# A feed-forward up product by seven products of quarters, with the down product in a stage of its own

## The chip, the cores and the metric

The kernel runs on one core of a Trainium2 chip. The metric is the time of one execution on the device in microseconds (us). The engines of the core work side by side, each through its own queue in order: TensorE (PE) multiplies, VectorE (DVE), ScalarE (ACT) and GpSimd (POOL) work elementwise, and SyncE (SP) issues the DMAs. A matmul holds one 128x128 block of weights, loaded just before it (PEld in the profile), and streams the columns of the other operand through it. Results come up in PSUM and are taken from there to SBUF by DVE or ACT.

## The reference

One layer of a hybrid decoder, in float32: an mLSTM branch, an SSD branch, a merge, a LayerNorm, and a feed-forward part with a short causal convolution. The change touches only the last part (1056 token columns after the cut of the meta tokens, width 1024, inner width 2816):

```python
x1 = layer_norm(ALPHA * x + mixed, w['ln1_g'], w['ln1_b'])
up = x1 @ w['w_up']                                   # 1024 -> 2 * 2816
upc, fconv_new = causal_dwconv(up, fconv_buf, w['w_fconv'], w['b_fconv'])
ff = (jax.nn.silu(upc[..., :D_FF]) * upc[..., D_FF:]) @ w['w_down']
x2 = layer_norm(ALPHA * x1 + ff, w['ln2_g'], w['ln2_b'])
```

The layer's output x2 and all convolution and recurrent states are returned.

## The kernel before

Features lie on the 128 partitions and tokens in the free dimension. A float32 operand enters a product as a pair: `hi` is the value rounded for the multiplier (an ACT copy, line 141), `lo` the rest (a DVE subtraction, line 142). Each block product is three matmuls, hi·hi, lo·hi and hi·lo (`mm3`, lines 156 to 158), each with its own weight load.

The normalised activations x1 stand as eight pairs `x1h`, `x1l` (one for each block of 128 features), 1058 columns wide, cut into three column tiles of 354, 352 and 352 (`NTC`). The feed-forward part runs over 22 pairs of units: `act_tile(i)` takes up unit i (the gated half) and unit 22 + i (the other half). An up unit loads a 128x1024 block of `w_up`, splits it into `whi`, `wlo`, and does 3 column tiles x 8 feature blocks x 3 = 72 matmuls; ACT copies the result from PSUM (`gps`) to `u`. Then the convolution runs along the tokens: one ACT pass (line 1092) and two DVE passes (line 1094) a unit; tanh on ACT (line 1104), one DVE pass for the silu (line 1105), and the product of both halves on DVE (lines 1110 and 1111). The result is split at once into `ah`, `al` (`split` in `act_tile`) and kept in SBUF.

The down product runs between the up units. `FPARTS` cuts the 22 activation tiles into parts of 3 or 2; as soon as a part is there, `down` multiplies it with its block of `w_down` into eight output tiles `mix` (`acc`), and after each part DVE adds the PSUM result to them (`down_evac`, 192 additions of 352 columns). A pair that is computed while `down` of the part ahead runs keeps PE supplied. The last part ends with the second LayerNorm. POOL does only small copies in this stage (lines 1075, 1088, 1089). The order on each queue follows the order of the code, except that weight loads (`wload`, `wdn`) are pulled ahead by `WAHEAD` instructions; `wst`, `whi` and `wlo` have two buffers each.

Of the kernel before, what the change touches and what calls it, by code (L numbers as in the profile page):

```python
# [34 lines left out]
FPARTS = [3, 3, 3, 3, 3, 2, 2, 3]  # L35
# [11 lines left out]
def kernel(ctx, tc, I, O):  # L47
# [8 lines left out]
    dr = ctx.enter_context(tc.tile_pool(name="dr", bufs=1, space=DRAM))  # L56

# [12 lines left out]
    rd = dr.tile([4, TC], F32, name="rd")  # L70
    negMd = dr.tile([4, T], F32, name="negMd")
# [19 lines left out]
    maskA = const.tile([NA, NA], F32, name="maskA")  # L91
# [13 lines left out]
    bm = const.tile([96, NB], F32, name="bm")  # L105
# [8 lines left out]
    tk1 = const.tile([128, 9, 12], F32, name="tk1")  # L114
    tk2 = const.tile([128, 9, 96], F32, name="tk2")
    mdec = const.tile([128, 4, 16], F32, name="mdec")
    sdec = const.tile([128, 32, 16], F32, name="sdec")
# [785 lines left out]
    pp = ctx.enter_context(tc.tile_pool(name="pp", bufs=1))  # L903
# [5 lines left out]
    def ptile(dt, nm, w=TC):  # L909
        return pp.tile([128, PW], dt, tag="P", name=nm, bufs=22)[:, 0:w]  # L910

    def pair(src, mul=None):
        f = ptile(F32, "pf")
        dma(f, src)
        if mul is not None:
            V.tensor_tensor(f, f, mul, ALU.mult)
        return pair_of(f)

    def pair_of(f):
        hi, lo = ptile(F32R, "ph"), ptile(F32R, "pl")  # L920
        split(hi, lo, f)
        return hi, lo
# [6 lines left out]
    xp_cm.__exit__(None, None, None)  # L929

    qp_ = ctx.enter_context(tc.tile_pool(name="qmix", bufs=1, side="right"))
    mix = [qp_.tile([128, TC], F32, name=f"mix{m}") for m in range(8)]
    with ExitStack() as c3:
        q2 = c3.enter_context(tc.tile_pool(name="q2", bufs=2, side="right"))

        def gate_tile(m):
            t = q2.tile([128, TC], F32, tag="gt", name="gt")
            dma(t, gd[m])
            return t

        def w3(nm, *ix, **kw):
            src = I[nm]
            for i in ix:
                src = src[i]
            return wload(src.rearrange("p (k c) -> p k c", c=128), **kw)

        def gemms(unit, rhs):
            gemm_wide([unit(0), unit(1)], NTC, rhs)
            for m in range(2, 7):
                w, evac = unit(m)  # L950
                gemm(w, NTC, rhs, evac, KD, gps if m % 2 else rps)
            gemm_wide([unit(7)], NTC, rhs)

        def unit_a(m):
            w = w3("wpa", m, scale=mg)
            gt = gate_tile(m)

            def evac(j, t0, n, ps, gt=gt, m=m):
                V.scalar_tensor_tensor(mix[m][:, t0:t0 + n], gt[:, t0:t0 + n], 1.0, ps, op0=ALU.add, op1=ALU.mult)
            return w, evac  # L960
        gemms(unit_a, prhs(hp))
        for half in range(2):
            yp = []
            for k in range(8):
                if k % 4 == 0:
                    R = q2.tile([128, TC], F32, tag="R", name="R")
                    gi = half * 2 + k // 4
                    dma(R, rd[gi:gi + 1].rearrange("o t -> (o t)").partition_broadcast(128))
                yp.append(pair(yd[half * 8 + k], mul=R))

            def unit_b(m):
                w = w3("wpb", m, half, scale=sg[:, half * 8:half * 8 + 8])
                gt = gate_tile(8 + m)

                def evac(j, t0, n, ps, gt=gt, m=m):
                    tmp = q2.tile([128, 354], F32, tag="tmp", name="tmp")
                    V.scalar_tensor_tensor(tmp[:, 0:n], gt[:, t0:t0 + n], 1.0, ps, op0=ALU.add, op1=ALU.mult)
                    V.tensor_tensor(mix[m][:, t0:t0 + n], mix[m][:, t0:t0 + n], tmp[:, 0:n], ALU.add)
                return w, evac
            gemms(unit_b, prhs(yp))  # L980
    mpair = [pair_of(mix[k]) for k in range(8)]
    x1x = ctx.enter_context(tc.tile_pool(name="x1x", bufs=1, side="right"))

    def x1tile(k, nm):
        return ptile(F32R, nm) if k < 3 else x1x.tile([128, TC], F32R, name=f"{nm}{k}")

    with ExitStack() as c3:
        q3 = c3.enter_context(tc.tile_pool(name="q3", bufs=2, side="right"))
        x1p = [(x1tile(k, "x1h"), x1tile(k, "x1l")) for k in range(8)]
        def unit_out(m, t0, n, s1=None):  # L990
            w = wload(I["wout"][m].rearrange("p (k c) -> p k c", c=128))
            xr = q3.tile([128, 354], F32, tag="tmp", name="xr")
            dma(xr[:, 0:n], xd[m, :, t0:t0 + n])

            def evac(_, t0, n, ps):
                r = mix[m][:, t0:t0 + n]
                V.scalar_tensor_tensor(r, ps, 0.5 / ALPHA, xr[:, 0:n], op0=ALU.mult, op1=ALU.add)
                if m:
                    G.tensor_tensor(s1[:, 0:n], mix[0][:, t0:t0 + n] if m == 1 else s1[:, 0:n], r, ALU.add)
            return w, evac  # L1000

        def parts(n):
            return [(a, min(128, n - a)) for a in range(0, n, 128)]

# [92 lines left out]
    def act_tile(i):  # L1097
# [8 lines left out]
        if i:  # L1106
            next(ub)
# [204 lines left out]
```

## Time and profile before

| | us |
|---|---|
| median of 3 runs (lowest to highest) | 2491.01 (2485.77 to 2493.09) |
| the profiled execution | 2483.84 |
| its span, first to last instruction | 2481.9 |
| PE busy in the span | 2410.1 |
| DVE busy | 1464.1 |
| ACT busy | 837.5 |
| POOL busy | 382.4 |
| from the first matmul on x1 (1664.5) to the last (2386.7) | 722.2 |

A matmul's busy time reaches from its start to its modelled end and overlaps the next one's. What a matmul costs is read from the distance of starts. Idle time of an engine is put down to the instruction that released it.

### The profile page before, as it was taken

What the parts mean: (1) busy time and instruction counts of PE and PEld (TensorE: products, weight loads), DVE (VectorE), ACT (ScalarE), POOL (GpSimd) and SP (SyncE); (2) the same over time, 40 slices, a digit from 0 to 9 for tenths busy, and PEclk for the clock granted to TensorE, in tenths of its full rate; (3) what the DMA queues carried; (4) which work ended last, traced back from release to release, by engine and by line L of the source; (5) the groups of instructions that cost most, each with busy time, mean ns of one, the idle gap of its engine ahead of it and who ended that gap; (6) DMA issues with size and microseconds to landing.
All of it is one profiled execution on the core that took longest, in us unless ns stands there. A gap on an engine that the chain in (4) does not pass through costs nothing.

```text
span 2481.9 us, 37118 instructions
## 1 busy us (share of the span) xinstructions
PE 2410.1 (97%) x14835; PEld 2300.5 (93%) x14835; DVE 1464.1 (59%) x2449; ACT 837.5 (34%) x1631; POOL 382.4 (15%) x475
## 2 busy tenths in 40 slices
PE   7999999999999999999979999999999999999996
PEld 6898998989999899899979999989999999999995
DVE  7647666567457657654444755686544545445458
ACT  6243332544324424433221211354232323323321
POOL 0010000233123223222000000231010101101104
PEclk9999999999999999999989999999999999999998
DMA  9233332234443353344243433441111111111121
GB/s 245 70 107 116 116 98 85 74 118 113 113 163 75 98 163 74 98 144 118 91 170 132 165 113 104 143 143 40 49 40 50 43 52 44 49 48 44 49 56 70
DMA packets 161853, 241.02 MB, mean 97 GB/s; under 512 B 37433, under 2 KB 117145, under 8 KB 161681
## 3 DMA queue, kind: packets, MB, share of 16 engines
q1 hardware_dynamic: 161680, 238.66, 31.8%
q8 instruction: 116, 1.90, 0.3%
q14 instruction: 57, 0.46, 0.1%
HBM read 188.54 MB, written 50.07 MB: 96 GB/s over the span
## 4 chain that ended last, share of the span: by engine, by line
PE 72%; DVE 3%; DMA 3%; ACT 1%; POOL 1%; issue 0%; SPq 0%; ACTq 0%; POOLq 0%; DVEq 0%
PE gps L156 17%; PE gps L158 17%; PE gps L157 17%; PE rps L158 5%; PE rps L156 5%; PE rps L157 5%; PE rps L787 1%; PE rps L797 1%; PE rps L806 1%; DMA s<-in_s0T 1%; PE rps L713 1%; POOL sqa L1020 1%; DMA out_sS<-s 1%; ACT whi L141 0%; PE rps L749 0%; DMA pf<-yd 0%
## 5 line engine op out<-in xcount | busy, mean ns | idle before, releaser
L156 PE MATMUL gps<-xh,whi 128*128 128x352 f32 (+4 forms) x1752 | 590.8, 337 | 0.0
L157 PE MATMUL gps<-xl,whi 128*128 128x352 f32 (+4 forms) x1752 | 572.8, 327 | 0.0
L158 PE MATMUL gps<-xh,wlo 128*128 128x352 f32 (+4 forms) x1752 | 572.5, 327 | 0.0
L142 DVE TENSOR_TENSOR wlo<-wst,whi 128x1024 fp32r<-128x1024 f32 (+2 forms) x205 | 250.1, 1222 | 404.8 <-ACT whi L141 404.6
L141 ACT ACTIVATE whi<-wst 128x1024 fp32r<-128x1024 f32 (+2 forms) x205 | 207.6, 1015 | 603.8 <-PE gps L157 356.0
L156 PEld LDWEIGHTS gps<-xh,whi 128*128 128x128 f32 (+1 forms) x1752 | 330.7, 189 | 16.4 <-issue 12.4
L156 PE MATMUL gps<-x1h,whi 128*128 128x352 f32 (+1 forms) x1056 | 345.7, 327 | 0.0
L158 PE MATMUL gps<-x1h,wlo 128*128 128x352 f32 (+1 forms) x1056 | 343.7, 325 | 0.0
L157 PE MATMUL gps<-x1l,whi 128*128 128x352 f32 (+1 forms) x1056 | 343.5, 325 | 0.0
L157 PEld LDWEIGHTS gps<-xl,whi 128*128 128x128 f32 (+1 forms) x1752 | 331.0, 189 | 12.5 <-issue 11.8
L158 PEld LDWEIGHTS gps<-xh,wlo 128*128 128x128 f32 (+1 forms) x1752 | 330.1, 188 | 1.1 <-issue 1.0
L158 PEld LDWEIGHTS gps<-x1h,wlo 128*128 128x128 f32 x1056 | 200.6, 190 | 0.1
L157 PEld LDWEIGHTS gps<-x1l,whi 128*128 128x128 f32 x1056 | 200.3, 190 | 0.0
L156 PEld LDWEIGHTS gps<-x1h,whi 128*128 128x128 f32 x1056 | 199.5, 189 | 0.3 <-ACT whi L141 0.2
L156 PE MATMUL gps<-ph,whi 128*128 128x352 f32 (+1 forms) x472 | 151.9, 330 | 9.6 <-ACT ph L141 7.0
L157 PE MATMUL gps<-pl,whi 128*128 128x352 f32 (+1 forms) x472 | 154.5, 327 | 0.0
L158 PE MATMUL gps<-ph,wlo 128*128 128x352 f32 (+1 forms) x472 | 153.4, 326 | 0.0
L708 ACT ACTIVATE dec<-dec,tk 128x128 f32<-128x128 f32 (+1 forms) x288 | 90.3, 383 | 175.8 <-POOL dec L705 153.6
L158 PE MATMUL rps<-ah,wlo 128*128 128x352 f32 x456 | 147.6, 324 | 0.0
L156 PE MATMUL rps<-ah,whi 128*128 128x352 f32 x456 | 147.3, 323 | 0.0
L157 PE MATMUL rps<-al,whi 128*128 128x352 f32 x456 | 147.2, 323 | 0.0
L1119 DVE SCALAR_TENSOR_TENSOR mix<-rps,mix 128x352 f32<-128x352 f32 x168 | 85.3, 521 | 68.7 <-PE rps L158 68.7
(362 smaller groups left out, 4122.9 us busy)
## 6 DMA issues: line engine op xcount, KB each, us to landing
wst<-in_win SPq DMA_DIRECT2D x72, 512.0 KB, 3.7
wst<-in_wup SPq DMA_DIRECT2D x44, 512.0 KB, 3.3
dec<-btd SPq DMA_DIRECT2D x32, 512.0 KB, 5.7
gt<-gd SPq DMA_DIRECT2D x24, 529.0 KB, 3.5
wst<-in_wout SPq DMA_DIRECT2D x24, 512.0 KB, 3.2
wst<-in_wdn SPq DMA_DIRECT2D x24, 384.0 KB, 3.5
yd<-xs SPq DMA_DIRECT2D x16, 529.0 KB, 3.9
pf<-yd SPq DMA_DIRECT2D x16, 529.0 KB, 5.8
```

The lines of the kernel that those rows point to most:

```text
L141: S.activation(hi, src, AF.Copy)
L142: V.tensor_tensor(lo, src, hi.bitcast(F32), ALU.subtract)
L156: PE.matmul(out, ah, bh, start=start, stop=False)
L157: PE.matmul(out, ah, bl, start=False, stop=False)
L158: PE.matmul(out, al, bh, start=False, stop=stop)
L708: S.activation(dec[:n, i, 0:n], dec[:n, i, 0:n], AF.Exp, bias=tk2[:n, c, g * 8 + i:g * 8 + i + 1], scale=1.0)
L713: PE.transpose(xps[:n, i * 128:(i + 1) * 128], xc, ident)
L787: PE.matmul(iv[(i % 2) * 64:(i % 2) * 64 + 64, i // 2, 0:n], xdt[:n, i, :], dec[:n, i, 0:n], start=True, stop=True)
L797: PE.matmul(ev_[:, i, :], St[:, i * 128:(i + 1) * 128], C[:, t0:t0 + n], start=True, stop=True)
L806: PE.matmul(aps, bt_, xw.rearrange("p h e -> p (h e)"), start=True, stop=True)
L1020: G.tensor_tensor(sqa[:, 0:n], sqa[:, 0:n], sq[:, 0:n], ALU.add)
L1119: V.scalar_tensor_tensor(a, ps, 1.0 / ALPHA, a, op0=ALU.mult, op1=ALU.add)
```

## The change

The first two pairs of units (`PLAIN = 2`) are computed as before. For the other 20 pairs the weights of a pair are a 2x2 arrangement of blocks (units i and 22 + i by the two halves of the 1024 features), and x1 a 2x2 arrangement (the halves of the features by two halves of the columns, `HC = 530` each). The pair then takes seven products of such quarters, in the Winograd form: each has 4 feature blocks x 3 matmuls on two column pieces (`HP`, 266 and 264), 168 matmuls a pair. Four products run on a combination of weights (`s1` to `s4`, four POOL operations of 128x512, then a split into `wf`), three on a piece of the weights itself (`a11`, `a12`, `a22`, split straight from the loaded block `raw`). Three run on combinations of x1, which are formed and split once (`tf`), between the LayerNorm and the first of the seven products. Three of the seven products accumulate in a PSUM bank in which another product already lies. The seven results are put together by ACT copies, DVE additions from PSUM and two POOL additions. Weights are prepared five products ahead (`AHEAD`), in six buffers `wf`. The convolution of pair i runs piecewise while pair i + 1 is multiplied (`act_steps`).

The loaded blocks `raw` are the four tiles that first hold the units of the plain pairs. The activations go to DRAM (`fd`) instead of being split at once, and x1 goes there too (`x1d`), since its tiles `mix` serve the new stage as work space. After all up units the down product runs alone: activations are loaded again and split (`act_load`), x1 is loaded into `acc`, and parts of 6, 6, 6 and 4 tiles follow each other, the last as before. The additions to `acc` fall from 192 to 96. Pools of SBUF are arranged anew (`pa`, `pb`, fixed tiles for what stood in `q2`, `q3`, `fp`; three buffers of `tmp`), and the merge's code ahead of the LayerNorm is the same work in other tiles.

```diff
-FPARTS = [3, 3, 3, 3, 3, 2, 2, 3]
+HC = 530
+HP = [(0, 266), (266, 264)]
+PLAIN = 2
+AHEAD = 5
+FPARTS = [6, 6, 6, 4]
...
+    for m in range(8):
+        dma(x1d[m], mix[m][:, 2:TC])
...
+    raws = [ptile(F32, "raw", PW) for _ in range(4)]
+    ca, cb, ta, sw1, sw2, X, uA, uB = mix_
...
+    plains = [plain(m, u) for m, u in zip((0, 22, 1, 23), raws)]
...
+    for k in range(4):
+        b11, b12 = mix_[k][:, 0:HC], mix_[k][:, HC:2 * HC]
+        b21, b22 = mix_[4 + k][:, 0:HC], mix_[4 + k][:, HC:2 * HC]
+        G.tensor_tensor(b11, b12, b11, ALU.subtract)
+        G.tensor_tensor(b12, b22, b12, ALU.subtract)
+        V.tensor_tensor(b22, b22, b11, ALU.subtract)
+        V.tensor_tensor(b21, b22, b21, ALU.subtract)
+        for f, t in enumerate((b11, b22, b12)):
+            split(tf[f][k // 2][0][:, k % 2], tf[f][k // 2][1][:, k % 2], t)
+    for k in range(4):
+        split(x1p[k][0][:, HC:2 * HC], x1p[k][1][:, HC:2 * HC], mix_[4 + k][:, 0:HC])
+    for i in range(PLAIN):
+        run(act_steps(i, *raws[2 * i:2 * i + 2]))
...
+    PRODUCTS = [("a11", half(0, 0)), ("s1", form(0)), ("s2", form(1)), ("s4", half(4, 1)),
+                ("a12", half(4, 0)), ("s3", form(2)), ("a22", half(0, 1))]
...
+    def prepare(n):
...
+        if p == 5 and i < 21:
+            up_load(i + 1)
...
+        if nm == "s1":
+            G.tensor_tensor(t, a21, a22, ALU.add)
+        elif nm == "s2":
+            G.tensor_tensor(t, sums["s1"], a11, ALU.subtract)
+        elif nm == "s4":
+            G.tensor_tensor(t, a12, sums["s2"], ALU.subtract)
+        else:
+            G.tensor_tensor(t, a11, a21, ALU.subtract)
+        split(h, l, t)
...
+    for i in range(PLAIN, 22):
+        for p, (nm, xf) in enumerate(PRODUCTS):
+            n = 7 * (i - PLAIN) + p
+            prepare(n + AHEAD)
...
+                    PE.matmul(ps, wh_, a, start=new and k == 0, stop=False, **chk)
+                    PE.matmul(ps, wh_, b, start=False, stop=False, **chk)
+                    PE.matmul(ps, wl_, a, start=False, stop=k == 3, **chk)
+                s1, s5 = X[:, j, 0:w_], X[:, 2 + j, 0:w_]
+                if p == 0:
+                    S.copy(s1, ps)
+                elif p == 1:
+                    S.copy(s5, ps)
+                elif p == 2:
...
+                    V.tensor_tensor(u2, ps, s1, ALU.add)
+                elif p == 3:
+                    V.tensor_tensor(uA[:, 16 + HC + t0:16 + HC + t0 + w_], ps, banks["u2", j], ALU.add)
+                elif p == 4:
+                    put_copy(uA, t0, w_, ps)
+                elif p == 5:
+                    V.tensor_tensor(s1, ps, s1, ALU.add)
+                    G.tensor_tensor(uB[:, 16 + HC + t0:16 + HC + t0 + w_], s1, s5, ALU.add)
+                else:
+                    put(lambda to, a, b, f: V.tensor_tensor(
+                        to, f(s1[:, a:b]) if f else s1[:, a:b], f(ps[:, a:b]) if f else ps[:, a:b],
+                        ALU.subtract), uB, t0, w_)
...
+    acc = [t[:, 0:TF] for t in (mix_[3:] + mix_[0:3])]
+    for m in range(8):
+        dma(acc[m], x1d[m])
...
+    for kk, nk in zip(FPARTS, FPARTS[1:]):
+        nxt = []
+        for m in range(8):
+            hi, lo = wdn(m, k0, kk, 1)
+            gemm((hi[:, 0], lo[:, 0]), NTF, prhs(acts), down_evac(m), kk, rps if m % 2 else gps)
+            if m < nk:
+                nxt.append(act_load(k0 + kk + m))
+        k0 += kk
+        acts = nxt
```

**TensorE, within the up product.** Each row is a line, an operation, its result and operands, and the columns. Before, two feature blocks at the end of one column tile of a unit:

```order
L156 MATMUL gps<-x1h_14795,whi 128x354
L157 MATMUL gps<-x1l_14796,whi 128x354
L158 MATMUL gps<-x1h_14795,wlo 128x354
L156 MATMUL gps<-x1h_14797,whi 128x354
L157 MATMUL gps<-x1l_14798,whi 128x354
L158 MATMUL gps<-x1h_14797,wlo 128x354
```

After, the end of the first product of the first pair (on x1 itself) and the start of the second (on a combination):

```order
L1253 MATMUL rps<-x1h,wf 128x264
L1254 MATMUL rps<-x1l,wf 128x264
L1255 MATMUL rps<-x1h,wf 128x264
L1253 MATMUL rps<-tf,wf 128x266
L1254 MATMUL rps<-tf,wf 128x266
L1255 MATMUL rps<-tf,wf 128x266
```

The kinds of matmul are the same three; each weight load now serves 264 or 266 columns instead of 352 or 354.

**VectorE, in the middle of the up units.** Before, one pair of units, from the split of its first weights to that of its result (`ca`, `cb`: the two convolutions):

```order
L142 TENSOR_TENSOR wlo<-wst,whi 128x1024
L1094 SCALAR_TENSOR_TENSOR ca<-u,c_fcw,ca 128x1072 x2
L1105 SCALAR_TENSOR_TENSOR ca<-ta,ca 128x1072
L142 TENSOR_TENSOR wlo<-wst,whi 128x1024
L1094 SCALAR_TENSOR_TENSOR cb<-u,c_fcw,cb 128x1072 x2
L1110 TENSOR_TENSOR ta<-ca,cb 128x1024
L1111 TENSOR_TENSOR ta<-ca,cb 128x32
L142 TENSOR_TENSOR al<-ta,ah 128x1056
```

After, half a pair, from the second convolution of the pair ahead to the put-together of the fourth product (L153 is the split, L1119 the convolution, L1130 the product of the halves):

```order
L153 TENSOR_TENSOR wf<-mix,wf 128x512
L1119 SCALAR_TENSOR_TENSOR mix<-mix,c_fcw 128x1072
L153 TENSOR_TENSOR wf<-raw,wf 128x512
L1119 SCALAR_TENSOR_TENSOR mix<-mix,c_fcw 128x1072
L1130 TENSOR_TENSOR mix<-mix 128x1024
L153 TENSOR_TENSOR wf<-raw,wf 128x512
L1131 TENSOR_TENSOR mix<-mix 128x32
L1264 TENSOR_TENSOR tmp<-rps,mix 128x266
L1264 TENSOR_TENSOR tmp<-gps,mix 128x264
L153 TENSOR_TENSOR wf<-mix,wf 128x512
L1266 TENSOR_TENSOR mix<-rps,tmp 128x266
L1266 TENSOR_TENSOR mix<-rps,tmp 128x264
```

The splits of weights are cut in seven smaller ones a pair, the split of the result is gone from this stage, and additions from PSUM stand between the convolutions.

**GpSimd, one pair.** Before, it had three copies a unit (lines 1075, 1088, 1089) and nothing else in this stage. After, one pair of units:

```order
L1215 TENSOR_TENSOR mix<-raw 128x512
L1113 COPY so<-mix 128x2
L1217 TENSOR_TENSOR mix<-mix,raw 128x512
L1114 COPY so<-mix 128x16
L1219 TENSOR_TENSOR mix<-raw,mix 128x512
L1271 TENSOR_TENSOR mix<-mix 128x266
L1271 TENSOR_TENSOR mix<-mix 128x264
L1113 COPY so<-mix 128x2
L1106 COPY mix<-si 128x8x2
L1114 COPY so<-mix 128x16
L1221 TENSOR_TENSOR mix<-raw 128x512
L1106 COPY mix<-si 128x8x2
```

Six operations with two operands in SBUF are new; the six copies of a pair remain.

**VectorE, from the combinations of x1 to the first weights of the seven products** (after only; before, the splits of x1 are followed by the weights and convolutions of the first units):

```order
L1164 TENSOR_TENSOR mix<-mix 128x530
L153 TENSOR_TENSOR tf<-mix,tf 128x530 x2
L1165 TENSOR_TENSOR mix<-mix 128x530
L153 TENSOR_TENSOR tf<-mix,tf 128x530 x2
L1119 SCALAR_TENSOR_TENSOR mix<-raw,c_fcw,mix 128x1072 x4
L1126 SCALAR_TENSOR_TENSOR mix<-mix 128x1072
L1130 TENSOR_TENSOR mix<-mix 128x1024
L1131 TENSOR_TENSOR mix<-mix 128x32
L153 TENSOR_TENSOR wf<-raw,wf 128x512
L1119 SCALAR_TENSOR_TENSOR mix<-raw,c_fcw,mix 128x1072
L153 TENSOR_TENSOR wf<-raw,wf 128x512
```

The first split of the new weights (`wf`) stands behind the combinations and behind the whole convolution of plain pair 0, whose tiles `raw` the weights are loaded into.

## Rows read from the trace of the kernel before

**Rows 1.** The page: busy time and share of the engines; the chain.

```profile
PE 2410.1 (97%) x14835; PEld 2300.5 (93%) x14835; DVE 1464.1 (59%) x2449; ACT 837.5 (34%) x1631; POOL 382.4 (15%) x475
...
PE 72%; DVE 3%; DMA 3%; ACT 1%; POOL 1%; issue 0%; SPq 0%; ACTq 0%; POOLq 0%; DVEq 0%
```

**Rows 2.** Windows: width, busy PE, PEld, DVE, ACT, POOL (count), clock, DMA share, GB/s.

```profile
1700.00:2000.00 300.00, 300.00 (x1850) 300.00 (x1849) 149.83 (x169) 93.97 (x156) 34.88 (x54) 1.00 0.17 47
2000.00:2300.00 300.00, 300.00 (x1850) 300.00 (x1849) 144.46 (x176) 86.97 (x145) 29.65 (x49) 1.00 0.16 47
...
2430.00:2482.00 52.00, 28.09 (x160) 25.94 (x158) 46.83 (x138) 11.67 (x16) 28.10 (x21) 0.76 0.22 84
```

**Rows 3.** Timeline, TensorE: start, duration, engine, line, operation; nine matmuls of 512 columns.

```profile
100.03 0.40 PE L158 MATMUL gps<-whi,xl 128*128 128x512 f32 x1
...
101.90 0.40 PE L157 MATMUL gps<-wlo,xh 128*128 128x512 f32 x1
```

**Rows 4.** The page: a weight load's mean; timeline: loads before short matmuls.

```profile
L158 PEld LDWEIGHTS gps<-x1h,wlo 128*128 128x128 f32 x1056 | 200.6, 190 | 0.1
...
193.41 0.54 PEld L588 LDWEIGHTS rps<-vs,ksm 96*128 96x128 f32 x4 [0.40 <-issue]
...
743.83 2.02 PEld L858 LDWEIGHTS rps<-ones,u 128*34 128x34 f32 x18 [0.23 <-issue]
```

**Rows 5.** Groups by form, DVE: busy us, mean ns, then idle before.

```profile
L1094 DVE SCALAR_TENSOR_TENSOR ca<-u,c_fcw,ca 128x1072 f32<-128x1072 f32 x44 | 58.7, 1335 | 14.1 <-ACT ca L1092 13.3
...
L1110 DVE TENSOR_TENSOR ta<-ca,cb 128x1024 f32<-128x1024 f32 x22 | 26.9, 1222 | 0.5
...
L603 DVE SCALAR_TENSOR_TENSOR C<-C,mdec,rps 128x257 f32<-128x257 f32 x32 | 14.9, 466 | 0.0
...
L142 DVE TENSOR_TENSOR wlo<-wst,whi 128x512 fp32r<-128x512 f32 x8 | 5.5, 691 | 16.5 <-ACT whi L141 16.5
...
L1042 DVE TENSOR_TENSOR mix<-mix,rps 128x352 f32<-128x352 f32 x16 | 7.5, 514 | 0.6 <-PE rps L1039 0.6
...
L1111 DVE TENSOR_TENSOR ta<-ca,cb 128x32 f32<-128x32 f32 x22 | 4.1, 184 | 0.0
```

**Rows 6.** Groups by form, POOL.

```profile
L774 POOL TENSOR_TENSOR s<-s,sdec 128x512 f32<-128x512 f32 x32 | 37.4, 1197 | 60.1 <-PE rps L749 60.1
L705 POOL TENSOR_SCALAR_AFFINE_SELECT dec<-dec 128x1024 f32<-128x1024 f32 x32 | 36.6, 1143 | 81.8 <-DMA dec<-btd 79.5 <-PE gps L158 2.2
...
L1075 POOL COPY u<-si 128x16 f32<-128x16 f32 x44 | 9.8, 223 | 2.3 <-DMA si<-in_fcs 2.3
...
L999 POOL TENSOR_TENSOR s<-s,mix 128x354 f32<-128x354 f32 x6 | 5.7, 948 | 18.3 <-DVE mix L997 18.3
```

**Rows 7.** Timeline, POOL: two operations side by side with DVE.

```profile
562.00 1.06 POOL L807 TENSOR_TENSOR S<-S,sdec 128x512 f32<-128x512 f32 x1 [4.07 <-DVE S L809]
563.01 2.08 POOL L705 TENSOR_SCALAR_AFFINE_SELECT dec<-dec 128x1024 f32<-128x1024 f32 x1
```

**Rows 8.** Timeline, DVE, the same stretch, operands in SBUF alone.

```profile
561.93 2.20 DVE L500 SCALAR_TENSOR_TENSOR xs<-u,cv 128x16 f32<-128x16 f32 x2
564.06 1.07 DVE L501 SCALAR_TENSOR_TENSOR xs<-u,cv 128x32 f32<-128x32 f32 x1
```

**Rows 9.** Timeline, DVE: operands from PSUM, then a split.

```profile
1634.57 3.10 DVE L1013 SCALAR_TENSOR_TENSOR mix<-rps,mix 128x352 f32<-128x352 f32 x7
1638.16 1.62 DVE L142 TENSOR_TENSOR wlo<-wst,whi 128x1024 fp32r<-128x1024 f32 x1 [0.49 <-ACT whi L141]
```

**Rows 10.** Timeline, POOL, at the time of the last group.

```profile
1635.70 7.95 POOL L1020 TENSOR_TENSOR sqa<-sqa,sq 128x352 f32<-128x352 f32 x7 [4.26 <-ACT sq L1015]
```

**Rows 11.** Windows, matmuls that read x1h alone, until the LayerNorm's last split.

```profile
1664.00:1691.00 27.00, 19.36 (x73) 12.76 (x73) 3.99 (x8) 3.48 (x8) 1.00 0.13 41
```

**Rows 12.** The page: DMA rate in 40 slices; a weight block's landing (KB, us).

```profile
GB/s 245 70 107 116 116 98 85 74 118 113 113 163 75 98 163 74 98 144 118 91 170 132 165 113 104 143 143 40 49 40 50 43 52 44 49 48 44 49 56 70
...
wst<-in_wup SPq DMA_DIRECT2D x44, 512.0 KB, 3.3
```

More of the change, by code (lines that the diff above doesn't have):

```diff
@@ L929 @@
     xp_cm.__exit__(None, None, None)
[L931 to L956, printed above, removed]
+    rc_cm.__exit__(None, None, None)
@@ new lines, with btile, tmp_tile @@
+    pb = ctx.enter_context(tc.tile_pool(name="pb", bufs=20, side="right"))
+    sm = ctx.enter_context(tc.tile_pool(name="sm", bufs=2, side="right"))
+    def btile(dt, nm, w=TC):
+        return ptile(dt, nm, w, pb)
+    mix_ = [btile(F32, "mix", PW) for m in range(8)]
+    for t in mix_:
+        G.memset(t[:, TC:2 * HC], 0.0)
+    mix = [t[:, 0:TC] for t in mix_]
+    def tmp_tile():
+        return sm.tile([128, 354], F32, tag="tmp", name="tmp", bufs=3)
+    gts, Rs, pfs = ([btile(F32, nm) for _ in range(n)] for nm, n in (("gt", 3), ("R", 2), ("pf", 3)))
@@ L958, in evac @@
             def evac(j, t0, n, ps, gt=gt, m=m):
-                V.scalar_tensor_tensor(mix[m][:, t0:t0 + n], gt[:, t0:t0 + n], 1.0, ps, op0=ALU.add, op1=ALU.mult)
+                tmp = tmp_tile()
+                V.scalar_tensor_tensor(tmp[:, 0:n], gt[:, t0:t0 + n], 1.0, ps, op0=ALU.add, op1=ALU.mult)
+                V.tensor_tensor(mix[m][:, t0:t0 + n], mix[m][:, t0:t0 + n], tmp[:, 0:n], ALU.add)
             return w, evac
[L961 to L980, printed above, removed]
@@ new lines, in parts, with center @@
+    def parts(n):
+        return [(a, min(128, n - a)) for a in range(0, n, 128)]
+    def center(t0, n, s1, summed):
+        mu = rps()
+        PE.matmul(mu[:, 0:n], ones, s1[:, 0:n], start=True, stop=True)
+        vps = None if summed else [rps() for _ in parts(n)]
+        sqa = sm.tile([128, 354], F32, tag="sqa", name="sqa", bufs=1) if summed else None
+        for m in range(8):
+            r = mix[m][:, t0:t0 + n]
+            V.scalar_tensor_tensor(r, mu[:, 0:n], -1.0 / 1024, r, op0=ALU.mult, op1=ALU.add)
+            sq = sqa if summed and m == 0 else tmp_tile()
+            S.activation(sq[:, 0:n], r, AF.Square)
+            if not summed:
+                for (a, w_), vp in zip(parts(n), vps):
+                    PE.matmul(vp[:w_, 0:1], sq[:, a:a + w_], ones[:, 0:1], start=m == 0, stop=m == 7)
+            elif m:
+                G.tensor_tensor(sqa[:, 0:n], sqa[:, 0:n], sq[:, 0:n], ALU.add)
+        return sqa, vps
@@ new lines, with up_load @@
+    loads, forms = {}, {}
+    sums = {nm: (sw1, sw2)[q // 2][:, 512 * (q % 2):512 * (q % 2) + 512].rearrange("p (k c) -> p k c", c=128)
+            for q, nm in enumerate(("s1", "s2", "s4", "s3"))}
+    wf = [wp.tile([128, 2, 4, 128], F32R, tag=t, name="wf") for t in ("wl", "ws", "wh") for _ in range(2)]
+    first = []
+    def up_load(i):
+        loads[i] = []
+        for m in (i, 22 + i):
+            st = raws[2 * (i % 2) + m // 22][:, 0:1024].rearrange("p (k c) -> p k c", c=128)
+            dma(st, up_w(m))
+            loads[i].append(st)
@@ L1116, in down_evac, with wdn @@
+    run(end)
+    while len(first) < FPARTS[0]:
+        first.append(act_load(len(first)))
+    acc = [t[:, 0:TF] for t in (mix_[3:] + mix_[0:3])]
+    for m in range(8):
+        dma(acc[m], x1d[m])
     def down_evac(m):
         def evac(j, t0, n, ps):
-            a = acc[m][:, 2 + t0:2 + t0 + n]
+            a = acc[m][:, t0:t0 + n]
             V.scalar_tensor_tensor(a, ps, 1.0 / ALPHA, a, op0=ALU.mult, op1=ALU.add)
         return evac
-    def wdn(m, k0, kk, pool, tag, bufs):
+    def wdn(m, k0, kk, mm):
@@ L1211 @@
                 norm_begin()
[L1212 removed]
+        while otiles and otiles[0][0] + otiles[0][1] <= nt[0] + nt[1]:
             ready.append(otiles.pop(0))
```

355 lines of the change are left out of this document (209 added, 146 removed).

## The prediction

> **What bounds the kernel now.** I read the page first: PE is busy 97% of the span, and the chain of work that ended last is 72% PE [rows 1]. Then the stretches [rows 2]: from 1700 us on, through all up and down products, PE has no idle time (300.00 of 300), while DVE is half busy (149.83 and 144.46) and POOL does little. Only the tail has idle PE, and the change leaves the tail's work as it was. So the feed-forward part is as long as its matmuls are, and what a matmul costs is the first question.
>
> Its busy time does not answer that, since matmuls overlap. 1850 of them, nearly all with 352 columns, start in 300 us [rows 2]: 162.2 ns each. With 512 columns eight starts take 1.87 us [rows 3], 233.8 ns each. That is 0.461 and 0.457 ns per column: the cost goes with the columns, though each matmul has its own weight load. How short a matmul may get before the weight load sets its pace is in [rows 4]: 18 loads before 34-row products with few columns took 2.02 us, at most 112 ns each. Four before products of 258 columns took 0.54 us from the first start to the last end; a load of this size lasts 0.19, so that three distances are 0.35 us, 117 ns each. For 265 columns I take 265 x 0.460 = 121.9 ns; 120 (117 x 265 / 258) and 123.3 ns (a straight line through 352 and 512 columns) are the bounds, all over the 112.
>
> The Trainium skill, "TensorE: Matmul & The Clock Gate", section "Back-to-back issue gap", gives other figures for a stream of weight loads and matmuls: 81 ns with 128 columns, 131 ns with 512. By it (an estimate, on a straight line) 352 columns would cost 110 ns and 265 columns 99 ns, and the up product would grow by 15 us instead of shrinking. The row with 512 columns shows 233.8 ns, so the sum goes by the rows.
>
> **The change, part by part.**
>
> *Matmuls of the up product.* Before: 44 units x 72 = 3168, at 162.2 ns 513.9 us. After: 4 plain units, 288 x 162.2 = 46.7 us, and 20 pairs x 168 = 3360 x 121.9 = 409.6 us. Together 456.3: **-57.6 us**; with 120 and 123.3 ns -64 and -53. The down product keeps its 1584 matmuls of 352 columns.
>
> *The rest of a pair's work.* One pair now has 168 x 121.9 = 20.5 us of PE. What the other engines must do in it, by [rows 5] and [rows 6]:
> DVE: seven splits of 512 columns (0.691), 4.8 us; five passes over 1072 columns (1.335), 6.7; the product of the halves, 1.222 + 0.184, 1.4. These 12.9 us read SBUF alone. From PSUM come seven pieces of some 265 columns (0.466 at 257, 0.514 at 352: 0.47) and two short ones (0.184 each), 3.7. Sum 16.6 us, 81% of PE's time, where it was half.
> POOL: four operations of 512 columns (1.06 alone in [rows 7], 1.197 as a mean), two of 265 (0.948 x 265 / 354 = 0.71), six copies (0.223): 7.0 to 7.5 us.
> ACT gets some 10 us; it was busy a third of the time [rows 2] and stays off the path.
> Each engine alone would fit in. But DVE and POOL do not run freely side by side. In [rows 7] and [rows 8], from 561.93 to 565.13, POOL's 1.06 us and 1.14 us (the usual time of the second, [rows 6]) and DVE's passes over 16, 1024 and 32 columns (0.18 + 1.22 + 0.18 by forms of the same length, [rows 5]) would take 3.8 us one after another and 1.6 to 2.2 side by side; they took 3.2, the second POOL operation 2.08 instead of 1.14, and the 32 columns of DVE 1.07 instead of 0.18. So operations with operands in SBUF alone nearly exclude each other. With operands from PSUM they do not: seven of those took 3.10 us [rows 9] while POOL ran [rows 10], 0.44 each, and the split behind them took 1.62 instead of 1.222 [rows 5].
> What must go one by one in a pair is then 12.9 + 7.0 to 7.5 = 19.9 to 20.4 us, and the 3.7 us from PSUM lie beside POOL's or not: 19.9 to 24.1, against PE's 20.5. The weights are five products (14.6 us) ahead, so that bunching within a pair is smoothed; an average over 20.5 is not. Back-to-back rows show starts some 0.08 us closer than durations (3.10 / 7 = 0.44 in [rows 9] against 0.514 for the same length in [rows 5]), which takes 1 us from DVE's sum. I take a mean of 21.0, 0.5 us over PE's, since most of the PSUM pieces find a POOL operation to lie beside: **+10 us** over 20 pairs, from 0 to +72 (24.1).
>
> The Trainium skill, "GPSIMD Engine Reference", section "Key points", says that GpSimd shares its SBUF interfaces with VectorE and that contention arises with DVE instructions with two SBUF inputs. Rows 7 to 10 agree; it is the rule that speaks against this change, and the first rival below is what it would make of the sum.
>
> *From the LayerNorm to the seven products.* The combinations of x1 need its last split, at about 1691. By then 73 matmuls that read x1h have run [rows 11], two in three of the up product's, so 110 of the plain units' 288 are done, and the other 178 last 28.9 us, until 1720. In that time POOL has 8 operations of 530 columns (1.1 to 1.3) and DVE 20 of 530 (some 0.71, from the row of 512) and two plain splits (1.22), which all exclude each other: 25.4 to 27 us, until 1717. The weights for the seven products land in the tiles `raw` that hold the plain units, and only after the convolution of pair 0 has read them: 4 x 1.335 = 5.3 us, until 1722. Behind that come the load (3.3 us, [rows 12]) and the first split (0.63 on ACT by my estimate from DVE's, 0.69 on DVE): 1727. The second and third product need a POOL sum and a split each (1.06 + 0.7 + 0.7), in a queue that the second convolution shares: some 4 us more of gaps. PE idles **+11 us**; 3 if half of the combinations were formed while the LayerNorm's last splits ran, 20 if they queue behind x1's splits and the convolution of pair 1. SP's queue carries the eight stores to `x1d` (4.3 MB) ahead of those loads; at the 245 GB/s of the first slice [rows 12] they are over 18 us after 1691 and hide.
>
> *From the seven products to the down product.* The convolution and product of pair 21 and the reload and split of the last activations come before the first part can end; the first block needs its six tiles, of which five can be loaded in time. Stores and loads of `fd`, 2 x 11.9 MB, x1 back (4.3 MB), and `w_down` as before; in the first 70 us of the stage about 14 MB, 200 GB/s, under the 245 seen. 7 to 8 us of DVE and DMA latency stand in a row, about half of which the first five tiles' matmuls cover: **+4 us**, 0 to 12.
>
> *Down stage and the rest.* A part of six has 54 matmuls a unit, 8.75 us, in which DVE does one split of 768 columns, three additions (0.514) and a split of an activation (about 1.3): 4 us. No bound there: 0. The additions saved (96 x 0.514) were hidden. New pools in the merge, three `tmp`: 0 ± 4.
>
> Sum: -57.6 + 10 + 11 + 4 = -32.6 us on the profiled execution, 2483.84 - 32.6 = 2451.2. That execution lay 7.2 us under the median of the runs shown, so against the median **2458 us**.
>
> **The rivals.**
>
> *DVE and POOL become the bound (slower).* If the PSUM pieces find nothing to lie beside, a pair lasts 23.5 to 24.1 us: 20 x 3.0 to 3.6 = 60 to 72 us, and with 15 us at the two borders the time is 2491 - 57.6 + 75 to 87 = 2508 to 2520. It decides from (57.6 - 15) / 20 = 2.1 us, that is from a cycle of 22.6. For it: [rows 7] and [rows 8], and a queue of 22 DVE operations that wait for ACT and POOL in turn. Against it: seven operations from PSUM ran at 0.44 us beside POOL. Chance 0.16.
>
> *All of it is hidden.* POOL's operations lie in DVE's waits and beside its PSUM pieces; a pair lasts 20.5 us, and the borders cost 5. Then 2491 - 57.6 + 5 = 2438. For it: 19.9 is under 20.5, and starts are closer than durations. Chance 0.22.
>
> *The borders cost twice as much.* 20 and 12 us and the 10 of the pairs: 2491 - 57.6 + 42 = 2475. Chance 0.10.
>
> *A matmul does not shrink with its columns.* At 139 ns each the up product is as long as before, and the time 2491 + 25 = 2516. For it: the 0.35 us of [rows 4] hold only three distances, in a place that PE shared with other products. Two lengths on one line through zero [rows 2, 3] speak against it. Chance 0.03.
>
> **How the numbers follow.** My forecast, a pair at 20.5 to 21.6 us and borders of 10 to 20, spans 2446 to 2472 and has 0.49. A measurement of this kernel can tell about 0.3% from no change, 7.5 us: faster is under 2483.5, slower over 2498.5. Faster: 0.49 + 0.22 + 0.05 of the border case = 0.76. Same: the rest of the border case and the milder part of the first rival, 0.08. Slower: 0.16. The range takes in the hidden case and the larger part of what lies between the forecast and the first rival: 2434 to 2506.
>
> **What the profile after would show.** In the middle of the up stage, 168 starts in 20.5 us (121.9 ns each) and no idle PE if the cycle is PE's; if it is DVE's, PE idles before the products' matmuls, waiting for splits `wf` or a bank that L1264, L1266 or L1270 reads, with DVE busy over 95%. DVE's splits of 512 columns would read about 0.9 instead of 0.691 and POOL's operations about 1.5 instead of 1.06. A gap of some 11 us in PE stands near 1720, ended by the split of `wf`, and one of some 4 us before the first down matmul, ended by the split of an activation. The forecast is wrong if matmuls are further apart than 124 ns without a wait, or if PE idles over 1 us in each pair.

## The result and the profile after

The changed kernel takes 2450.85 us (median of four, 2447.88 to 2452.53), the kernel before 2488.75 (median of four runs by then). The ratio is 0.9846, interval 0.9829 to 0.9863: 1.5% faster, 38 us. The forecast was 2458, range 2434 to 2506.

The page, busy time and share, then the share of DVE and POOL in 40 slices:

```profile
PE 2360.0 (96%) x15315; PEld 2244.2 (92%) x15315; DVE 1580.7 (65%) x2673; ACT 874.3 (36%) x1703; POOL 577.4 (24%) x611
...
DVE  7656667567457757755446456477988888874338
...
POOL 0010000233123223222100000044655655410004
```

Against [rows 1] PE lost 50 us of busy time, DVE gained 117 and POOL 195, nearly all in slices 28 to 36, where the combinations of x1 and the seven products stand. Windows of the changed kernel, columns as in [rows 2]:

```profile
1735.00:1760.00 25.00, 20.41 (x143) 19.98 (x142) 21.50 (x26) 11.68 (x22) 16.97 (x14) 0.86 0.34 108
1760.00:1900.00 140.00, 140.00 (x1139) 140.00 (x1138) 118.99 (x166) 66.16 (x120) 85.11 (x82) 1.00 0.25 83
1900.00:2100.00 200.00, 200.00 (x1626) 200.00 (x1625) 165.80 (x231) 96.44 (x176) 119.30 (x119) 1.00 0.24 77
```

From 1760 us to the down product (2156) PE has no idle time, with DVE at 83 to 85% and POOL at 60% until 2100. The pair's length is read from one line that runs once a pair, the silu pass L1126 (number of times, shortest, median and longest ns, first and last start):

```profile
L1126 DVE SCALAR_TENSOR_TENSOR mix<-mix x11: 1259/1261/1265, 1827.1 to 2034.0; 128x1072 f32<-128x1072 f32 x11
```

Ten pairs in 206.9 us, 20.69 each, 123.1 ns for each of 168 matmuls.

Where the 36.1 us between the two profiled spans (2481.9 and 2445.8) went, from the starts of the stages' first matmuls:

| stretch | before | after | difference | forecast |
|---|---|---|---|---|
| until the merge's first matmul | 1273.1 | 1275.2 | +2.2 | 0 |
| merge and LayerNorm, to the first matmul on x1 | 391.5 | 400.3 | **+8.8** | 0 ± 4 |
| first 288 matmuls on x1 | 55.7 | 59.4 | +3.7 | with the next but one |
| rest of the up product: its matmuls (2880 x 162.2, 3360 x 123.1 ns) | 467.1 | 413.6 | **-53.5** | -57.6 |
| the same: what else it took | - | 7.8 | +7.8 | 11 with the 3.7 above |
| the pairs beyond PE's time | - | 0 | **0** | +10 |
| down product and second LayerNorm | 294.6 | 289.5 | **-5.1** | +4 |

In before the 289th matmul on x1 starts at 1720.3. The down product's matmuls lie between those of the up product there, so its last row is what is left of the span. The total is within 3.5 us of the forecast (-36.1 for -32.6) because larger errors cancel: the pairs were forecast 10 and the end 9 too dear, the merge 9, the matmuls 4 and the start 2 too cheap.

### The profile page after: what moved, and what is told of

It is laid out like the page before. It is cut to its first block, busy times and chain, and to the rows that moved or that the text cites. A ratio compares the mean times of both kernels' runs of the same rounds, so it can differ in the third digit from the quotient of the medians.

```text
span 2445.8 us, 38900 instructions
## 1 busy us (share of the span) xinstructions
PE 2360.0 (96%) x15315; PEld 2244.2 (92%) x15315; DVE 1580.7 (65%) x2673; ACT 874.3 (36%) x1703; POOL 577.4 (24%) x611
## 5 line engine op out<-in xcount | busy, mean ns | idle before, releaser
L152 ACT ACTIVATE whi<-wst 128x1024 fp32r<-128x1024 f32 (+1 forms) x161 | 164.6, 1023 | 501.6 <-PE gps L168 305.0
L153 DVE TENSOR_TENSOR wlo<-wst,whi 128x1024 fp32r<-128x1024 f32 (+1 forms) x161 | 199.7, 1242 | 178.4 <-ACT whi L152 178.0
L1254 PE MATMUL rps<-x1l,wf 128*128 128x266 f32 (+1 forms) x480 | 137.3, 286 | 0.0
L1253 PE MATMUL rps<-x1h,wf 128*128 128x266 f32 (+1 forms) x480 | 137.3, 286 | 0.0
L1255 PE MATMUL rps<-x1h,wf 128*128 128x266 f32 x480 | 136.7, 285 | 0.0
L1119 DVE SCALAR_TENSOR_TENSOR mix<-mix,c_fcw 128x1072 f32<-128x1072 f32 x80 | 115.9, 1448 | 6.9 <-ACT mix L1117 6.9
L167 PEld LDWEIGHTS gps<-ph,whi 128*128 128x128 f32 x472 | 88.9, 190 | 19.5 <-ACT ph L152 16.0
L506 DVE SCALAR_TENSOR_TENSOR cv<-u,c_scw,cv 128x1096 f32<-128x1096 f32 x72 | 97.7, 1357 | 8.7 <-ACT cv L504 7.4
L167 PE MATMUL gps<-ah,whi 128*128 128x352 f32 x312 | 101.1, 325 | 0.0
L169 PE MATMUL gps<-ah,wlo 128*128 128x352 f32 x312 | 100.9, 323 | 0.0
L168 PE MATMUL gps<-al,whi 128*128 128x352 f32 x312 | 100.6, 323 | 0.0
```

Of the source, the lines that this page charges most:

```text
L152: S.activation(hi, src, AF.Copy)
L153: V.tensor_tensor(lo, src, hi.bitcast(F32), ALU.subtract)
L167: PE.matmul(out, ah, bh, start=start, stop=False)
L168: PE.matmul(out, ah, bl, start=False, stop=False)
L169: PE.matmul(out, al, bh, start=False, stop=stop)
L506: V.scalar_tensor_tensor(cv, u[:, j:j + 1096], cw[:, j:j + 1], cv, op0=ALU.mult, op1=ALU.add)
```

## Experiments

Six kernels were run once, on the same chip as one run of the kernel before: `pool_twice`, `dve_extra`, `hp354` and `tail3` (2486.65 before), `split_twice` and `psum_twice` (2488.44 before). The others, `plain22`, `hd_first`, `late` and `both`, were run 4 to 10 times, beside 13 runs of it (2487.71). Differences from the changed kernel are taken from its 2450.85.

**The rest of the change without the seven products.** All pairs plain:

```diff
-    for q in range(4):
-        run(plains[q])
...
+    for i in range(22):
+        for h in range(2):
+            run(plains[2 * i + h])
+        run(act_steps(i, *raws[2 * (i % 2):2 * (i % 2) + 2]))
```

> All 22 pairs are plain: the seven products, their weight sums and the combinations of x1 are gone, and the rest of the change stays (pools, x1 and activations in DRAM, the down product as a stage of its own, parts of 6, 6, 6 and 4). It measures that rest alone. Theory by the ledger of the two profiles: 11 us more ahead of the feed-forward part, 5 us less behind it, the up product 513.9 us again: 2488.75 + 11 - 5 = 2495, within 2488 to 2502, that is 0 to 0.5% slower than before. Rival (the stage of its own gains by itself): under 2480.

Measured 2498.48 us, ratio 1.0036 (1.0024 to 1.0048): slower than before, as expected. The restructuring around the seven products costs 0.4%; the products give 1.9% (0.9846 against 1.0036), 47 us.

**Does GpSimd's work stand in VectorE's way?** Four kernels add work to a pair of the changed one, with the same results. First, each weight sum twice on GpSimd:

```diff
             G.tensor_tensor(t, a21, a22, ALU.add)
+            G.tensor_tensor(t, a21, a22, ALU.add)
```

> Each of the four weight sums of a pair is computed twice on GpSimd (the second time into the same place with the same values), four more operations of 512 columns a pair, 1.3 us each, 5.2 us. Theory (operations of GpSimd and VectorE on SBUF alone go one by one, and a pair of the changed kernel, 20.69 us, is filled by them to about 18 to 19 us): the sum of what must go one by one passes 20.7, a pair lasts 22.5 to 24 us, TensorE gets idle time in each pair, and the kernel is 35 to 65 us slower than the changed one, near 2490 to 2515 us. Rival (both engines run freely side by side, only each one's own sum counts: VectorE 16.6, GpSimd 7.3 + 5.2): no pair is longer, within 3 us of the changed kernel's 2451.

Second, the repeated sum on VectorE instead (`V` for the added `G`):

> Each of the four weight sums of a pair is computed on GpSimd and then once more on VectorE into the same place, four more VectorE operations of 512 columns a pair, 0.69 us each, 2.8 us. Theory (one by one on SBUF alone, with about 2 us left in a pair): a pair gets 0.5 to 1.5 us longer, 10 to 30 us in all, 2461 to 2481 us. Rival (free side by side; VectorE 19.4 of 20.7): within 3 us of 2451. Together with the kernel that doubles the sums on GpSimd it tells whether the time one by one counts or GpSimd's own chain of sums.

Third, six of the seven splits' subtractions twice:

```diff
         split(h, l, t)
+        V.tensor_tensor(l, t, h.bitcast(F32), ALU.subtract)
```

> The changed kernel, but six of the seven VectorE splits of a pair's weights are done twice, into the same place with the same values, right after one another: six more operations of 512 columns on SBUF alone, 0.62 us from start to start, 3.7 us a pair. GpSimd's work is as in the changed kernel. Theory (operations on SBUF alone go one by one with GpSimd's; bare, they take 18.7 us of a pair's 20.69): 22.4 us one by one, a pair lasts 22.0 to 22.9 us, 26 to 44 us more in all. Rival (each engine's own sum counts; VectorE from start to start 15.4 + 3.7 = 19.1): a pair stays at 20.69 and the time within 5 us of 2451. The earlier kernel with four extra sums on VectorE does not tell, since each of those waits for GpSimd's sum and holds VectorE's queue (3.6 us a pair).

Fourth, the additions from PSUM again (L1264 and L1273 twice, L1266 three times):

```diff
                     V.tensor_tensor(u2, ps, s1, ALU.add)
+                    V.tensor_tensor(u2, ps, s1, ALU.add)
```

> The changed kernel, but VectorE's additions from PSUM are repeated with the same values: those of the third product once more, of the fourth twice more, of the seventh once more, eight more pieces of 232 to 266 columns and two short ones, 0.35 to 0.42 us from start to start, 3.0 to 3.5 us a pair, nearly as much VectorE time as in the kernel with doubled splits. Theory (an operand from PSUM does not stand in GpSimd's way): they lie beside GpSimd's operations, VectorE's own sum is 18.4 to 18.9, a pair stays at 20.7 to 21.0 us and the time within 8 us of 2451. Rival (any VectorE operation stands in GpSimd's way): 22 us a pair as with doubled splits, 26 us or more in all.

The silu pass again, of these four in this order:

```profile
L1126 DVE SCALAR_TENSOR_TENSOR mix<-mix x10: 1551/1565/1575, 1828.6 to 2039.2; 128x1072 f32<-128x1072 f32 x10
```

```profile
L1126 DVE SCALAR_TENSOR_TENSOR mix<-mix x10: 1260/1264/1266, 1825.4 to 2031.8; 128x1072 f32<-128x1072 f32 x10
```

```profile
L1126 DVE SCALAR_TENSOR_TENSOR mix<-mix x10: 1261/1264/1268, 1823.6 to 2032.5; 128x1072 f32<-128x1072 f32 x10
```

```profile
L1126 DVE SCALAR_TENSOR_TENSOR mix<-mix x12: 1259/1262/1264, 1809.6 to 2036.9; 128x1072 f32<-128x1072 f32 x12
```

Nine, nine, nine and eleven pairs: 23.40, 22.93, 23.21 and 20.66 us each. The times are 2510.35, 2498.43, 2504.07 and 2449.24 us; the first and the last as the theory expected, the second and the third longer than its range. The windows from 1800 to 2100 of the third and the fourth:

```profile
1800.00:2100.00 300.00, 276.31 (x2159) 273.53 (x2159) 299.10 (x387) 122.55 (x233) 148.32 (x154) 0.97 0.22 72
```

```profile
1800.00:2100.00 300.00, 300.00 (x2439) 300.00 (x2437) 282.52 (x495) 143.59 (x261) 172.25 (x178) 1.00 0.25 78
```

With doubled splits DVE is busy 299.1 of 300 us: it has become the bound, though its own added work (3.7 us) on 16.6 would fit in 20.7. With nearly as much added work on PSUM operands (3.0 to 3.5 us) PE stays without idle time. So the kind of operand decides: operations on SBUF alone wait for GpSimd's and the other way round, those from PSUM do not. Taking the added 3.7 from 23.21 leaves, as an estimate, 19.5 us that the changed kernel's pair needs one by one, against PE's 20.69: about 1.2 us of room, where 2 were expected (so the doubled splits cost 53 us, not 26 to 44). The same subtraction on the first kernel (5.2 from 23.40) gives 18.2, but there DVE is busy 273.9 of 300 us and not full; so the room is known only as 1.2 to 2.5 us. The second kernel, dve_extra, tells less: each added sum waits for GpSimd's, in order, with DVE idle (253.8 of 300 busy), and it was past its expected 2481.

**Columns and weight loads.**

```diff
-HP = [(0, 266), (266, 264)]
+HP = [(0, 354), (354, 176)]
```

> The two column pieces of a product are 354 and 176 instead of 266 and 264, the same columns in the same number of matmuls. If a matmul costs its columns and nothing else, a pair stays at 20.7 us and the time within 5 us of 2451. If a weight load of 128 columns sets a floor of 107 to 112 ns under a short matmul (176 columns would take 81 to 83), a pair takes 84 x 163 ns + 84 x 107 to 112 ns = 22.7 to 23.1 us, 40 to 48 us more in all, near 2491 to 2499 us.

(The work tile of the results is laid out to match.) The timeline on PE, the twelve short matmuls of a product and the next wide one:

```profile
1901.42 0.25 PE L1252 MATMUL rps<-x1h,wf 128*128 128x176 f32 x1
1901.51 0.28 PE L1253 MATMUL rps<-x1l,wf 128*128 128x176 f32 x1
1901.62 0.27 PE L1254 MATMUL rps<-x1h,wf 128*128 128x176 f32 x1
...
1902.62 0.27 PE L1254 MATMUL rps<-x1h,wf 128*128 128x176 f32 x1
1902.73 0.36 PE L1252 MATMUL rps<-tf,wf 128*128 128x354 f32 x1
```

Ten distances from 1901.51 to 1902.62: 111 ns each for 176 columns, not 81. That is the pace of the weight loads in [rows 4] (at most 112 ns), so a weight load is taken to set it here; on the line of the longer matmuls (4.7 ns + 0.447 a column, from 352 and 512) it would be reached at some 240 columns, by estimate. The pair took 23.0 us as expected, the kernel 2512.31, 13 more than expected: beside the 46 us of the pairs, its first matmul on x1 stood 6 us later than in the changed kernel (the same code, see below), and PE waited 3.7 and 5.9 us at the end of the products.

**The merge.** SyncE in the changed kernel (start, length, line, transfer, count):

```profile
1273.38 0.48 SPq L992 DMA_DIRECT2D pf<-yd  x1
1273.90 2.93 SPq L1105 DMA_DIRECT2D si<-in_fcs  x3
1277.85 0.33 SPq L925 DMA_DIRECT2D pf<-hd  x1
1279.13 0.33 SPq L1105 DMA_DIRECT2D si<-in_fcs  x1
1280.83 0.33 SPq L992 DMA_DIRECT2D pf<-yd  x1
1282.21 0.33 SPq L925 DMA_DIRECT2D pf<-hd  x1
1288.22 0.80 SPq L992 DMA_DIRECT2D pf<-yd  x2
1289.38 0.32 SPq L925 DMA_DIRECT2D pf<-hd  x1
```

Three of the eight loads of `hd`, which the merge's first product needs, came earlier; loads of `yd` for the next product stand among the rest, and the last of `hd` is issued at 1296.86. Before, the same loads follow each other (the first of `hd` at 1267.97, then these):

```profile
1269.30 3.86 SPq L914 DMA_DIRECT2D pf<-hd  x7
1278.44 0.32 SPq L914 DMA_DIRECT2D pf<-yd  x1
```

`yd` goes into a ring of three fixed tiles, new in this change, and its loads wait there for the tile to be split; what is queued behind them waits too. The waits, of SyncE from 1262 to 1310, then of PE from 1255 to 1700:

```profile
SPq L992 <- DVE pl L153: 17.1, 3, 9.8
```

```profile
PE gps L167 <- ACT ph L152: 10.7, 4, 7.3
```

An order of issue on SyncE was the edit (the same for `R` and `si`):

```diff
-            dma(f, yd[half * 8 + k])
+            with tc.issue_after(hds[-1].ins):
+                dma(f, yd[half * 8 + k])
```

> The changed kernel, but the loads of yd and rd for the next product (and the up units' small si loads) are queued on SyncE behind the last load of hd. Theory: in the changed kernel the loads of yd into a ring of three tiles stand between those of hd and wait there for VectorE (17.1 us on SyncE), so that hd comes late and TensorE waits three more times between 1287 and 1302; with hd first these waits go, 5 to 8 us less than the changed kernel's 2451, 2443 to 2446. Rival (hd waits for free tiles of the smaller pool, 20 for 22): the waits stay, within 2 us of 2451.

Measured 2444.34 us, ratio 0.9821 (0.9806 to 0.9836). The three extra waits for `ph` are gone:

```profile
PE gps L167 <- ACT ph L152: 7.1, 1, 7.1
```

Merge and LayerNorm took 395.4 us here, 395.0 with both edits, 400.3 to 406.0 (median 403.7) in the nine kernels whose merge is as in the changed one, and 391.5 before. So the order of loads explains some 8 of 12 us. Of the other 4, 1 to 1.5 lie in the first 200 matmuls (35.8 and 35.6 us with the edit, 34.5 before; 42.6 in the changed kernel), whose first 10 us have a granted clock of 0.69 with the edit and 0.84 before; the rest stays open.

**From the LayerNorm to the seven products.** PE in the changed kernel:

```profile
1740.58 0.39 PE L1253 MATMUL rps<-tf,wf 128*128 128x266 f32 x1 [2.49 <-ACT wf L152]
1740.80 0.28 PE L1254 MATMUL rps<-tf,wf 128*128 128x266 f32 x1
1743.18 0.59 PE L1255 MATMUL rps<-tf,wf 128*128 128x266 f32 x1 [2.09 <-DVE wf L153]
1743.57 0.43 PE L1253 MATMUL rps<-tf,wf 128*128 128x266 f32 x1
1743.79 0.43 PE L1254 MATMUL rps<-tf,wf 128*128 128x266 f32 x1
```

The first product follows the plain pairs at once (1734.9 after 1734.8); the second waits twice (the expectation below says the second and the third), and after that matmuls of 266 columns stand 0.22 us apart, the lower of the clock's two levels (1.2 GHz), until 1748.6. The window from 1735 to 1760 has a granted clock of 0.86. The 23 matmuls at the lower level cost 23 x 0.097 = 2.2 us, with the two waits 6.8 of the 7.8 us. The edit defers work on VectorE ahead of the second product's weights:

```diff
-    for k in range(4):
-        split(x1p[k][0][:, HC:2 * HC], x1p[k][1][:, HC:2 * HC], mix_[4 + k][:, 0:HC])
-    for i in range(PLAIN):
-        run(act_steps(i, *raws[2 * i:2 * i + 2]))
+    run(act_steps(0, *raws[0:2]))
...
-    for n in range(AHEAD):
-        prepare(n)
+    for n in range(3):
+        prepare(n)
+    for k in range(4):
+        split(x1p[k][0][:, HC:2 * HC], x1p[k][1][:, HC:2 * HC], mix_[4 + k][:, 0:HC])
+    for n in range(3, AHEAD):
+        prepare(n)
+    run(act_steps(1, *raws[2:4]))
```

> The changed kernel, but between the combinations of x1 and the seven products the split of four pieces of x1 (needed only by the seventh product) and the convolution of the second plain pair are placed behind the weights of the first products. Theory: in the changed kernel the second and third product wait 2.5 and 2.1 us for VectorE, which does these things first, and TensorE then runs for some 6 us at the lower clock; without them 4 to 8 us less, 2443 to 2447. Rival (VectorE is full until then whatever the order): within 2 us of 2451.

Measured 2452.92 us, ratio 0.9859 (0.9838 to 0.9881): nothing gained. DVE's first split of a sum (`wf<-mix`) moved from 1742.45 to 1737.06, and PE did not follow. VectorE (the first of x1's four splits is at 1735.13), then PE:

```profile
1737.06 0.69 DVE L153 TENSOR_TENSOR wf<-mix,wf 128x512 fp32r<-128x512 f32 x1
1737.67 4.15 DVE L153 TENSOR_TENSOR x1l<-mix,x1h 128x530 fp32r<-128x530 f32 x3
1741.74 1.28 DVE L153 TENSOR_TENSOR wf<-mix,wf 128x512 fp32r<-128x512 f32 x2
```

```profile
1740.50 0.39 PE L1254 MATMUL rps<-tf,wf 128*128 128x266 f32 x1 [2.33 <-ACT wf L152]
1740.73 0.28 PE L1255 MATMUL rps<-tf,wf 128*128 128x266 f32 x1
1743.08 0.59 PE L1256 MATMUL rps<-tf,wf 128*128 128x266 f32 x1 [2.07 <-DVE wf L153]
```

Both waits end when the third split of a sum does, ACT's part first and DVE's at 1743.0, and the sums come one after another from GpSimd (1732.8 to 1740.6). But the edit did only part of what was meant: three of the four splits of x1 still run ahead of DVE's second and third split of a sum, 4.15 us beside GpSimd's sums. So this run does not tell whether GpSimd's sums or VectorE's order holds the start, and why PE waits for the third split is open.

**Both edits.**

> Both edits in one kernel: hd loaded first, and the split of x1 and the second convolution placed later. If they are independent, the sum of what each gives, 9 to 16 us less than the changed kernel, 2435 to 2442 us; if one only moves a wait to the next, no more than the larger of them.

Measured 2442.20 us, ratio 0.9809 (0.9792 to 0.9827). It is 46 us faster than the kernel before and 9 us faster than the changed one; from the first edit alone (2444.34) it can't be told, which agrees with the second giving nothing.

**The end.**

```diff
-FPARTS = [6, 6, 6, 4]
+FPARTS = [5, 5, 5, 4, 3]
```

> The parts of the down product are 5, 5, 5, 4 and 3 activation tiles instead of 6, 6, 6 and 4. What lies behind the seven products, down product and second LayerNorm, was 5 us shorter than before by the two profiles. Theory: that came from the last part, which has 4 instead of 3 tiles and so gives TensorE a third more work beside the LayerNorm of the first columns; with 3 it comes back, 3 to 6 us more than the changed kernel, with TensorE waiting longer for the LayerNorm's outputs at the end. Rival: it came from the down product as a stage of its own, and the time stays within 2 us of the changed kernel's.

Measured 2457.78 us in one run, 6.9 more than the changed kernel. The profiled spans differ by 10.3 us, of which 4.9 stand in the merge, whose code is the same. From the end of the last product on the profile has 294.8 us, 289.5 in the changed kernel and 294.6 before; 2.2 of the 5.3 are a wait ahead of the first down matmul. PE's waits at the end, of this kernel:

```profile
PE rps L1330 <- ACT o L1353: 10.1, 4, 5.7
PE gps L167 <- DVE mix L1295: 1.0, 1, 1.0
```

and of the changed kernel:

```profile
PE rps L1330 <- ACT o L1353: 4.4, 1, 4.4
PE rps L1330 <- DVE mix L1295: 2.4, 1, 2.4
PE rps L1330 <- DVE rs_y L138: 2.2, 1, 2.2
```

11.1 us with three tiles in the last part (10.1 before, 9.1 + 1.0), 9.0 with four. So the longer last part accounts for 2 to 3 us; the rest of the 5.1 isn't settled.

## Why the prediction was right, step by step

*Matmuls.* Right in kind. 123.1 ns lies on the straight line through 352 and 512 columns (123.3), the bound that was not taken, and not on the line through zero (121.9): each matmul has a fixed part of some 5 ns. On 3360 matmuls that is 4 us: -53.5 for -57.6.

*The pairs.* The mechanism was right, the term of 10 us was not: a pair lasts what PE needs, 20.69. This step put what goes one by one at 19.9 to 20.4 us and took a mean of 21.0, since only most of the PSUM pieces would find something to lie beside. No such cost is seen. The additions to a pair put the sum one by one at 18.2 to 19.5 us and show no cost of up to 3.5 us more from PSUM. This is the mechanism of the case "all of it is hidden" (2438), which failed only in the other terms. The waits of the two engines for each other are seen in the groups by form, 1760 to 2100:

```profile
L153 DVE TENSOR_TENSOR wf<-raw,wf 128x512 fp32r<-128x512 f32 x50 | 62.5, 1249 | 0.0
L153 DVE TENSOR_TENSOR wf<-mix,wf 128x512 fp32r<-128x512 f32 x65 | 45.2, 695 | 38.7 <-ACT wf L152 37.0
...
L1270 DVE TENSOR_TENSOR mix<-rps,mix 128x266 f32<-128x266 f32 x16 | 6.9, 434 | 2.6 <-PE rps L1255 2.6
```

```profile
L1221 POOL TENSOR_TENSOR mix<-raw 128x512 f32<-128x512 f32 x17 | 39.6, 2330 | 36.1 <-DVE wf L153 36.0
...
L1215 POOL TENSOR_TENSOR mix<-raw 128x512 f32<-128x512 f32 x16 | 20.9, 1306 | 32.5 <-DVE wf L153 30.1 <-DVE mix L1266 2.4
```

The mean of the 512-column splits is 0.94 us and that of GpSimd's sums 1.58, where the prediction named 0.9 and 1.5 as the sign of this mechanism. The same kind of split takes 695 ns or 1249 on average, the same kind of sum 1306 or 2330, by what stands beside it; an addition from PSUM takes 0.43. One place, GpSimd's sum beside a split, then a split with nothing beside it:

```profile
1870.46 2.32 POOL L1221 TENSOR_TENSOR mix<-raw 128x512 f32<-128x512 f32 x1 [2.25 <-DVE wf L153]
1871.55 1.78 DVE L153 TENSOR_TENSOR wf<-raw,wf 128x512 fp32r<-128x512 f32 x1
1875.75 0.69 DVE L153 TENSOR_TENSOR wf<-raw,wf 128x512 fp32r<-128x512 f32 x1
```

The first rival was real but had no room to act: the runs put its point at 1.2 to 2.5 us more work a pair on SBUF operands. By the rule of the Trainium skill on shared interfaces ("GPSIMD Engine Reference", "Key points") the collision was to be expected for operations with two SBUF inputs; the traces agree, and those with one input in PSUM, which that rule does not name, went free.

*The border to the seven products.* 11 us forecast, 11.5 measured (3.7 + 7.8), which is luck, since it did not come as the one gap of the forecast. The plain pairs ran 3.7 us longer, since x1's last four splits took 5.50 us beside GpSimd's combinations, at 0.52 us each alone, and PE waited for three of them; without the combinations (`plain22`) the same matmuls take 55.6 us. So the first weights came in time; then there were two short waits and the low clock, which the sum did not have. It had also left out the four splits of x1 that stand in the diff between the combinations and the seven products.

*The border to the down product, and the end.* 4 forecast, one wait of 1.7 us measured (DVE's second part of the first weights). The end is 5.1 us shorter all the same. The prediction says that the tail's work is as it was, but the last part grew from three tiles to four, which the runs put at 2 to 3 us.

*The merge.* The step that failed. "New pools in the merge, three `tmp`: 0 ± 4" cost 8.8: fixed rings let the loads of the next product be issued among those of the first, and on SyncE's queue they held back loads that PE waited for, some 8 us by the run `hd_first`. The order of SyncE, in which this stands, was not read there; only the stretches that the diff rewrites were.

*The forecast's own span.* By the prediction's figures a pair at 20.5 to 21.6 us and borders of 10 to 20 give 2443 to 2475, not 2446 to 2472; 2450.85 lies in either. That it lies so near the 2458 is in part luck, by the errors that cancel in the table above. The prediction's 112 ns for a weight load came from loads of 34 columns; `hp354` shows 111 for loads of 128.

## What to carry to other kernels

Where two engines do elementwise work beside each other, add up what each does on SBUF operands alone and compare that sum, not each engine's own, with the time that hides it; operations with one operand from PSUM were free of it here. Where a change turns a pool into a fixed ring, read the DMA queue's order: a load that waits for a ring's tile holds back every load behind it, also those of a stage that the change doesn't mean to touch. A product cut into narrower pieces pays by its columns down to the weight load's pace, here 111 ns.

## What the runs showed of the hardware

A matmul with its own weight load costs 111 ns with 176 columns, 123.1 with 265, 162.2 with 352 and 233.8 with 512. VectorE's and GpSimd's operations on SBUF alone waited for each other (a split of 512 columns 0.69 us alone and 1.78 beside a sum); VectorE's additions from PSUM did not (0.43). After two short waits of TensorE (2.5 and 2.1 us, with two matmuls between them) the matmuls ran at the lower level of the clock for about 5 us, which cost 2.2 us. Kernels with the same code up to the merge's end differed by up to 6 us in the time it took (400.3 to 406.0 from the merge's first matmul to the first on x1), so that a profile's difference of a few microseconds ahead of the edited place says nothing by itself.
